# A hand-written order for the first tokens of a SwiGLU: norms, block differences and first products on four engines

## The chip, the cores and the metric

The kernel runs on one core of a Trainium2 chip. The metric is the device time of one execution, in microseconds (us); the median of three runs stands for a kernel. A core has a matrix engine (TensorE, PE in the profile), a vector engine (VectorE, DVE), an activation engine (ScalarE, ACT), a general engine (GpSimd, POOL) and a queue that issues most of the transfers (SyncE, SP). Each engine works through its own list of instructions in the order in which the program holds them; engines wait for each other through semaphores.

## The reference, cut to what matters

One encoder layer on 1024 tokens of 1024 features. The change lies in the very first part, a SwiGLU of width 2816 behind an RMSNorm; the mixer and the second SwiGLU that follow are untouched.

```python
def rmsnorm(x, g):
    xf = x.astype(jnp.float32)
    y = xf * lax.rsqrt(jnp.mean(xf * xf, axis=-1, keepdims=True) + EPS)
    return (y * g.astype(jnp.float32)).astype(x.dtype)

def swiglu(x, w_gate, w_up, w_down):
    return (jax.nn.silu(x @ w_gate) * (x @ w_up)) @ w_down

def hybrid_layer(h, layer_idx, p):
    f = swiglu(rmsnorm(h, p["ffn1_pre_g"]), p["ffn1_w_gate"], p["ffn1_w_up"], p["ffn1_w_down"])
    h = h + 0.5 * rmsnorm(f, p["ffn1_post_g"])
    m = hybrid_mixer(rmsnorm(h, p["mix_pre_g"]), layer_idx, p)
    ...
```

## The kernel before, in words

Float32 operands are kept as two parts, a rounded one and the rest of it ("high" and "low"): `split` (L171 to L173) makes the high part on ACT and the low part by a subtraction on DVE, or on POOL where the caller names it. A product of two such operands is three matmuls (`mm3`, L178 to L180).

The first SwiGLU multiplies by blocks, with seven products in place of eight. The normed input has four blocks: first or last 512 tokens, first or last 512 features. For the seven products the kernel needs the transposed blocks b11 and b21 (both feature halves of the first 512 tokens), b22 (the last features of the last tokens) and four differences t1 to t4, which mix the blocks of first and last tokens. `blocks_prep` (L257) makes them, one tile of 128 tokens at a time. For every tile it loads x, squares and sums it on ACT and takes the power on POOL (`rstd`, L196 to L198), scales it on DVE (L264), transposes four 128x128 pieces at a time on PE (L270) and splits them. Tiles 0 to 3 have two such transposed groups (b11, b21). Tiles 4 to 7 have five (b22, t1 to t4) and before them four subtractions: t1 on POOL (L280), t2 on DVE (L281), t3 and t4 on POOL (L282, L283). The normed tiles 0 to 3 stay in two tiles of the weights' ring (`kept`); t1 and t2 lie in the two halves of the work tile w3, t3 and t4 in those of w4, x of tiles 4 to 7 takes turns in w0 and w1, and the gain lies in w2.

`begun` (called after tile 3) and `held` (after tiles 4 and 5) are the first products, those that need the first tokens alone. `begun` loads a weight tile of gate and one of up, splits each into two halves with the low parts on POOL, multiplies b11 by the first half, copies that sum out on ACT (`u`, L344), adds the product of b21 and the second half in the same bank of PSUM, and takes SiLU (L330) and the product with up (L334). `held` multiplies b11 by the first halves of the weight tiles 1 and 2, and leaves the four sums in their banks. One such product with a block is 12 matmuls of 128x512; all of these are 96. Transposes use banks 0 to 3 in turn.

Then the loop of `matrix` takes one weight tile pair after another: POOL adds and subtracts its quarters (L368 to L371), ACT and DVE split them, PE multiplies. Weight tiles come through three buffers for raw weights, so a load waits until the low part of an earlier tile has been made.

What sets the order: the program is built with a scheduler that follows a model of the engines' times, and places every instruction on its engine's list itself; the order of the Python calls only breaks ties. Nothing in the first SwiGLU is ordered by hand.

Of the kernel before, what the change touches and what calls it, by code (L numbers as in the profile page):

```python
# [17 lines left out]
F32 = mybir.dt.float32  # L18
# [3 lines left out]
ALU = mybir.AluOpType  # L22
# [3 lines left out]
P = 128  # L26
D = 1024
# [65 lines left out]
class Tags:  # L93


    def __init__(self, pool, n):
        self.pool, self.n = pool, n
        self.place = dict(x=(0, 2), gain=(2, 1), t0=(3, 1, 0), t1=(3, 1, 1), t2=(4, 1, 0), t3=(4, 1, 1))
        self.turn, self.made, self.half, self.next = {}, {}, None, 0

    def whole(self, i):
        return self.pool.tile([P, D], F32, tag=f"w{i}", name=f"w{i}", bufs=1)

    def tile(self, shape, dtype, tag, name, bufs):
        if tag == "rstd":
            return self.pool.tile(shape, dtype, tag=tag, name=name, bufs=bufs)
        if tag == "c":
            if self.half is None:
                self.half = self.whole(self.next % self.n)
                self.next += 1  # L110
                return self.half[:, 0:512]
            h, self.half = self.half, None
            return h[:, 512:1024]
        first, n, *part = self.place[tag]
        if not part:
            k = self.turn[tag] = (self.turn.get(tag, -1) + 1) % n
            return self.whole(first + k)
        if part[0] == 0:
            self.made[first] = self.whole(first)
        return self.made[first][:, part[0] * 512:(part[0] + 1) * 512]  # L120
# [17 lines left out]
class Kernel:  # L138
# [118 lines left out]
    def blocks_prep(self, tags, kept, junk, ps, src, gain, C, t):  # L257
# [44 lines left out]
    def blocks_gate_up(self, ring, cp, spool, ps, C, wg, wu, gd, early):  # L302
# [34 lines left out]
        def begun(i):  # L337

            for w in (wg, wu):
                r = raw(w[i])  # L340
                p = bank()
                u = spool.tile([P, 512], F32, tag="u", name="u", bufs=2)
                product(p, unit(r[:, 0:512], G), "b11")
                A.copy(out=u, in_=p)  # L344
                product(p, unit(r[:, 512:1024], G), "b21", True)
                first.append((u, None, None))
                if w is wg:
                    sg = gate11(p, spool.tile([P, 512], F32, tag="s", name="s", bufs=3))
                else:
                    up11(p, sg, i)  # L350

        def held(i, banks):

            for w, b in zip((wg, wu), banks):
# [4 lines left out]
                first.append((None, p, b))  # L359

# [948 lines left out]
def build(tc, a, out, stages="all"):  # L1309
    nc = tc.nc  # L1310
    with ExitStack() as top:
# [26 lines left out]
        with ExitStack() as c1:  # L1338
            ps = Banks(k.pool(c1, "ps1", space=PSUM))
            with ExitStack() as cb:  # L1340
# [7 lines left out]
                def early(begun, held):  # L1348
                    g = tags.tile([P, D], F32, "gain", "gain", 1)
                    nc.sync.dma_start(out=g, in_=a["ffn1_pre_g"].partition_broadcast(P))  # L1350
# [4 lines left out]

                    ps.turn = [0, 1, 2, 3]
# [191 lines left out]
```

## Time and profile before

| | |
|---|---|
| median of three runs | 2636.75 us (2634.49 to 2637.43) |
| the profiled execution's own time | 2636.05 us |
| its span, first to last instruction | 2634.3 us |
| PE busy | 2523.7 us (96%) |
| DVE, ACT, POOL busy | 1521.7, 1003.9, 825.1 us |
| mean granted clock of PE | 0.985 |

The profiled execution is 0.70 us under the median. PE is the busiest engine by far, so a stretch in which it waits, or in which it is granted the lower of its clocks, is what a change of order can move. In the profile's rows a time is counted from the span's start; a row gives the start, the duration, engine, line, operation, what is written and read, and in brackets how long the engine stood idle before it and what ended that. PEclk 1.00 is 2.4 GHz, 0.50 is 1.2 GHz.

### The profile page before, as it was taken

What the parts mean: (1) busy time and instruction counts of PE and PEld (TensorE: products, weight loads), DVE (VectorE), ACT (ScalarE), POOL (GpSimd) and SP (SyncE); (2) the same over time, 40 slices, a digit from 0 to 9 for tenths busy, and PEclk for the clock granted to TensorE, in tenths of its full rate; (3) what the DMA queues carried; (4) which work ended last, traced back from release to release, by engine and by line L of the source; (5) the groups of instructions that cost most, each with busy time, mean ns of one, the idle gap of its engine ahead of it and who ended that gap; (6) DMA issues with size and microseconds to landing.
All of it is one profiled execution on the core that took longest, in us unless ns stands there. A gap on an engine that the chain in (4) does not pass through costs nothing.

```text
span 2634.3 us, 32969 instructions
## 1 busy us (share of the span) xinstructions
PE 2523.7 (96%) x12504; PEld 2122.4 (81%) x12504; DVE 1521.7 (58%) x2123; ACT 1003.9 (38%) x1709; POOL 825.1 (31%) x750
## 2 busy tenths in 40 slices
PE   6999999999999999999979999999999999999996
PEld 4888888888888898877757888888888888888885
DVE  5765654564746553777737888888723333333336
ACT  5333222344535533454426555555531111111113
POOL 6432321020210484344326666666400000000005
PEclk8999999999999999999989999999999999999998
DMA  3322222765722575555464444441421111111112
GB/s 140 102 79 80 96 76 77 242 201 179 253 95 89 174 244 205 165 185 183 138 172 110 117 112 121 105 141 60 170 70 35 48 48 48 49 48 48 48 41 104
DMA packets 133694, 309.60 MB, mean 118 GB/s; under 512 B 13728, under 2 KB 62752, under 8 KB 128672
## 3 DMA queue, kind: packets, MB, share of 16 engines
q1 hardware_dynamic: 115200, 245.89, 28.3%
q0 software_dynamic: 10016, 57.42, 8.1%
q10 hardware_dynamic: 8320, 4.19, 0.5%
q8 instruction: 98, 1.61, 0.3%
q14 instruction: 60, 0.49, 0.1%
HBM read 228.02 MB, written 79.43 MB: 117 GB/s over the span
## 4 chain that ended last, share of the span: by engine, by line
PE 82%; DVE 6%; POOL 3%; ACT 3%; issue 2%; DMA 2%; SPq 0%; DVEq 0%; POOLq 0%; ACTq 0%
PE po L180 7%; PE po L178 7%; PE po L179 7%; PE b L178 5%; PE b L179 5%; PE b L180 5%; PE pp L178 5%; PE pp L180 5%; PE pp L179 5%; PE pg L178 3%; PE pg L179 3%; PE pg L180 3%; PE pu L179 3%; PE pu L178 3%; PE pu L180 3%
## 5 line engine op out<-in xcount | busy, mean ns | idle before, releaser
L197 POOL TENSOR_SCALAR rstd<-rstd 128x1 f32<-128x1 f32 x64 | 32.2, 503 | 986.8 <-ACT junk L196 985.8
L173 DVE TENSOR_TENSOR split<-raw,split 128x1024 fp32r<-128x1024 f32 (+3 forms) x218 | 250.3, 1154 | 128.4 <-ACT split L172 127.6
L172 ACT CAST split<-raw 128x1024 fp32r<-128x1024 f32 (+3 forms) x227 | 192.8, 860 | 231.0 <-issue 77.4
L502 DVE TENSOR_TENSOR acc<-acc,po 128x512 f32<-128x512 f32 x160 | 108.6, 686 | 209.6 <-PE po L180 209.5
L1046 ACT ACTIVATE e<-sc,st 128x1024 f32<-128x1024 f32 x128 | 143.4, 1120 | 165.4 <-DVE st L1042 165.4
L178 PE MATMUL pp<-hT,split 128*128 128x512 f32 x384 | 153.6, 400 | 10.2 <-DVE o L911 10.2
L1042 DVE TENSOR_REDUCE st<-sc 128x1 f32<-128x1024 f32 x128 | 150.6, 1217 | 12.6 <-PE sc L1040 12.6
L180 PE MATMUL pp<-hT,split 128*128 128x512 f32 x384 | 152.0, 396 | 0.0
L179 PE MATMUL pp<-hT,split 128*128 128x512 f32 x384 | 151.8, 395 | 0.0
L178 PE MATMUL po<-odd,g 128*128 128x512 f32 x352 | 139.0, 397 | 6.8 <-DVE acc L502 6.8
L180 PE MATMUL po<-odd,g 128*128 128x512 f32 x352 | 138.4, 395 | 0.0
L179 PE MATMUL po<-odd,g 128*128 128x512 f32 x352 | 138.2, 393 | 0.0
L178 PE MATMUL b<-hT,split 128*128 128x512 f32 x352 | 137.0, 390 | 0.0
L179 PE MATMUL b<-hT,split 128*128 128x512 f32 x352 | 136.9, 389 | 0.0
L180 PE MATMUL b<-hT,split 128*128 128x512 f32 x352 | 136.9, 389 | 0.0
L1053 POOL TENSOR_SCALAR e<-e,st 128x768 f32<-128x768 f32 x64 | 75.6, 1181 | 181.5 <-DVE st L1052 136.7
L179 PE MATMUL po<-split,gs 128*128 128x512 f32 x334 | 131.9, 395 | 0.0
L180 PE MATMUL po<-split,gs 128*128 128x512 f32 x334 | 131.9, 395 | 0.0
L178 PE MATMUL po<-split,gs 128*128 128x512 f32 x334 | 131.3, 395 | 0.0
L172 ACT CAST g<-sg 128x512 fp32r<-128x512 f32 (+1 forms) x52 | 28.8, 553 | 243.7 <-DVE acc L502 124.8
L1055 POOL TENSOR_TENSOR e<-e,e 128x768 f32<-128x768 f32 x64 | 118.3, 1848 | 5.4
L178 PE MATMUL pp<-split,hT 128*128 128x512 f32 (+1 forms) x320 | 117.5, 368 | 0.0
(378 smaller groups left out, 7246.7 us busy)
## 6 DMA issues: line engine op xcount, KB each, us to landing
raw<-in_w_down_dram SPq DMA_DIRECT2D x88, 512.0 KB
raw<-in_w_gate_dram SPq DMA_DIRECT2D x45, 512.0 KB
raw<-in_w_up_dram SPq DMA_DIRECT2D x45, 512.0 KB
qkd<-o SPq DMA_DIRECT2D x64, 256.0 KB
qk<-qkd POOLq DMA_DIRECT2D x16, 1024.0 KB, 7.8
gd<-w SPq DMA_DIRECT2D x42, 256.0 KB
vd<-o SPq DMA_DIRECT2D x32, 256.0 KB
kb<-qkd POOLq DMA_DIRECT2D x16, 512.0 KB, 5.2
```

Source lines behind the costliest of these rows:

```text
L172: self.nc.scalar.copy(out=hi, in_=src)
L173: (eng or self.nc.vector).tensor_tensor(out=lo, in0=src, in1=hi.bitcast(F32), op=ALU.subtract)
L178: mm(out=out, lhsT=a[0], rhs=b[0], start=start, stop=False, **kw)
L179: mm(out=out, lhsT=a[0], rhs=b[1], start=False, stop=False, **kw)
L180: mm(out=out, lhsT=a[1], rhs=b[0], start=False, stop=stop, **kw)
L197: nc.gpsimd.tensor_scalar(out=r[:, 1:2], in0=r[:, 0:1], scalar1=k / n, scalar2=k * EPS, op0=ALU.mult, op1=ALU.add)
L502: nc.vector.tensor_tensor(out=a[:, ns], in0=a[:, ns], in1=po[n], op=ALU.add)
L1042: nc.vector.tensor_reduce(out=X["st"][:, j:j + 1], in_=pc, op=ALU.max, axis=AX.X, negate=True)
L1046: self.nc.scalar.activation(out=X["e", j], in_=X["sc", j], func=AF.Exp, bias=st[:, j:j + 1], accum_out=st[:, 2 + j:3 + j])
L1053: G.tensor_scalar(out=e1[:, XD:], in0=e1[:, XD:], scalar1=st[:, 5:6], scalar2=0.0, op0=ALU.mult, op1=ALU.add)
L1055: G.tensor_tensor(out=e0[:, XD:], in0=e0[:, XD:], in1=e1[:, XD:], op=ALU.add)
```

## The change

Four things change. First, `blocks_prep` becomes a generator with two stops (after the norm's sums, and after the differences), its x is loaded by the caller, and the order of all calls is written out by hand inside `tc.manual_schedule` for PE, ACT, DVE and POOL; there the scheduler keeps the order of the calls. SP's queue is still the scheduler's. Second, `begun` is cut into load, begin, end and out, and `held` into its two products, and these stand between the tiles: gate's two products before the groups of tile 4, up's before those of tile 5, one of tile 1's products before tile 6 and the other before tile 7, the two of tile 2 behind tile 7. Third, the differences take the place of what they are made of: t1 and t4 overwrite the two halves of the kept tile, t3 the first half of x, and only t2 has a tile of its own. That leaves a third work tile for x. Fourth, the first tile of x is loaded ahead of the gain.

```diff
@@ class Tags
-        self.place = dict(x=(0, 2), gain=(2, 1), t0=(3, 1, 0), t1=(3, 1, 1), t2=(4, 1, 0), t3=(4, 1, 1))
-        self.turn, self.made, self.half, self.next = {}, {}, None, 0
+        self.place = dict(x=(0, 3), gain=(3, 1), t2=(4, 1))
+        self.turn, self.half, self.next = {}, {}, 0
...
@@ blocks_prep
-    def blocks_prep(self, tags, kept, junk, ps, src, gain, C, t):
+    def blocks_prep(self, tags, x, y, ps, gain, C, t, junk=None):
...
-        x = kept[t] if t < 4 else tags.tile([P, D], F32, "x", "x", 2)
-        nc.sync.dma_start(out=x, in_=src[t * P:(t + 1) * P, :])
-        r = self.rstd(tags, x, junk=junk())
+        r = self.rstd(tags, x, junk=junk and junk())
+        yield
         V.scalar_tensor_tensor(out=x, in0=x, scalar=r, in1=gain, op0=ALU.mult, op1=ALU.mult)
...
-        y = kept[t - 4]
-        t1, t2, t3, t4 = (tags.tile([P, 512], F32, f"t{i}", f"t{i}", 1) for i in range(4))
-        G.tensor_tensor(out=t1, in0=x0, in1=y[:, 0:512], op=ALU.subtract)
+        t1, t2, t3, t4 = y[:, 0:512], tags.tile([P, 512], F32, "t2", "t2", 2), x0, y[:, 512:1024]
+        G.tensor_tensor(out=t1, in0=x0, in1=t1, op=ALU.subtract)
         V.tensor_tensor(out=t2, in0=x1, in1=t1, op=ALU.subtract)
         G.tensor_tensor(out=t3, in0=x1, in1=x0, op=ALU.subtract)
-        G.tensor_tensor(out=t4, in0=y[:, 512:1024], in1=t2, op=ALU.subtract)
+        G.tensor_tensor(out=t4, in0=t4, in1=t2, op=ALU.subtract)
+        yield
         for n, v in (("b22", x1), ("t1", t1), ("t2", t2), ("t3", t3), ("t4", t4)):
             turn(n, v)
@@ blocks_gate_up
+            def load(self):
+                r = raw(self.w[self.i])
+                self.a11 = unit(r[:, 0:512], G)
+                self.a12 = unit(r[:, 512:1024], G)
+            def begin(self):
+                self.p = ps.at(4 if self.other is None else 5, [P, 512], "b")
+                self.u = spool.tile([P, 512], F32, tag="u", name="u", bufs=2)
+                product(self.p, self.a11, "b11")
+                A.copy(out=self.u, in_=self.p)
+                first.append((self.u, None, None))
+            def end(self):
+                product(self.p, self.a12, "b21", True)
...
@@ early
+                    xs = [load(0)]
                     g = tags.tile([P, D], F32, "gain", "gain", 1)
                     nc.sync.dma_start(out=g, in_=a["ffn1_pre_g"].partition_broadcast(P))
...
-                    for t in range(T):
-                        k.blocks_prep(tags, kept, junk, ps, a["x"], g, C, t)
-                        if t == 3:
-                            begun(0)
-                        elif t in (4, 5):
-                            held(t - 3, (2 * t - 4, 2 * t - 3))
+                    xs += [load(t) for t in range(1, 4)]
...
+                    with tc.manual_schedule(engines={E.PE, E.Activation, E.DVE, E.Pool}):
+                        for t in (0, 1, 0, 2, 1, 3, 2):
+                            step(t)
+                        gate, up = begun(0)
+                        gate.load()
+                        step(3)
+                        gate.begin()
+                        step(4)
+                        up.load()
+                        gate.end()
+                        for t in (5, 4):
+                            step(t)
+                        gate.out()
+                        step(4)
+                        up.begin()
+                        for t in (6, 5):
+                            step(t)
+                        up.end()
+                        step(5)
+                        up.out()
+                        for t in (7, 6):
+                            step(t)
+                        gate, up = held(1, (6, 7))
+                        gate()
+                        for t in (6, 7):
+                            step(t)
+                        up()
+                        step(7)
+                        for one in held(2, (4, 5)):
+                            one()
```

The change moves three lists where the prediction looks. In the lists below L173, L178 to L180, L196 to L198, L264, L270 and L280 to L283 of the kernel before are L175, L180 to L182, L198 to L200, L266, L272 and L281 to L284 of the changed one.

DVE at its first instructions, before: `split_111` and `split_112` hold the tiles 0 to 3, `hT0_98` is where b11 and b21 are split to, `pt` a transposed group.

```order
L264 SCALAR_TENSOR_TENSOR split_111<-split_111,rstd_115,w2_109 128x1024
L264 SCALAR_TENSOR_TENSOR split_111<-split_111,rstd_136,w2_109 128x1024
L264 SCALAR_TENSOR_TENSOR split_112<-split_112,rstd_157,w2_109 128x1024
L173 TENSOR_TENSOR hT0_98<-pt_120,hT0_98 128x4x128
L264 SCALAR_TENSOR_TENSOR split_112<-split_112,rstd_178,w2_109 128x1024
L173 TENSOR_TENSOR hT0_98<-pt_127,hT0_98 128x4x128
```

And DVE at the same place now.

```order
L266 SCALAR_TENSOR_TENSOR split_109<-split_109,rstd_120,w3_112 128x1024
L175 TENSOR_TENSOR hT0_98<-pt_130,hT0_98 128x4x128
L175 TENSOR_TENSOR hT0_98<-pt_137,hT0_98 128x4x128
L266 SCALAR_TENSOR_TENSOR split_109<-split_109,rstd_125,w3_112 128x1024
L175 TENSOR_TENSOR hT0_98<-pt_150,hT0_98 128x4x128
L175 TENSOR_TENSOR hT0_98<-pt_157,hT0_98 128x4x128
L266 SCALAR_TENSOR_TENSOR split_110<-split_110,rstd_145,w3_112 128x1024
```

The scaling of a tile now stands behind both low parts of the tile ahead of it; before, three tiles were scaled in a row.

POOL between the low parts of the first weights and the first difference, before: `split_201` and `split_237` are the weights of `begun`, `split_321` and `split_405` those of `held`, `w0` and `w1` the tiles 4 and 5.

```order
L173 TENSOR_TENSOR split_201<-raw_197,split_201 128x512 x2
L173 TENSOR_TENSOR split_237<-raw_233,split_237 128x512 x2
L173 TENSOR_TENSOR split_321<-raw_318,split_321 128x512
L173 TENSOR_TENSOR split_321<-raw_336,split_321 128x512
L173 TENSOR_TENSOR split_405<-raw_402,split_405 128x512
L173 TENSOR_TENSOR split_405<-raw_420,split_405 128x512
L197 TENSOR_SCALAR rstd_272<-rstd_272 128x1
L198 TENSOR_TENSOR rstd_272<-rstd_272,mhalf_65 128x1
L197 TENSOR_SCALAR rstd_356<-rstd_356 128x1
L198 TENSOR_TENSOR rstd_356<-rstd_356,mhalf_65 128x1
L280 TENSOR_TENSOR w3_277<-w0_269,split_111 128x512
```

And POOL now, from the norm of tile 7 (`rstd_376`) on: `w2_312` is tile 6, `w0_373` tile 7, `split_389` the weights of the first call of `held`.

```order
L199 TENSOR_SCALAR rstd_376<-rstd_376 128x1
L200 TENSOR_TENSOR rstd_376<-rstd_376,mhalf_65 128x1
L281 TENSOR_TENSOR split_110<-w2_312,split_110 128x512
L283 TENSOR_TENSOR w2_312<-w2_312 128x512
L284 TENSOR_TENSOR split_110<-split_110,w4_381 128x512
L175 TENSOR_TENSOR split_389<-raw_386,split_389 128x512
L281 TENSOR_TENSOR split_110<-w0_373,split_110 128x512
L283 TENSOR_TENSOR w0_373<-w0_373 128x512
L284 TENSOR_TENSOR split_110<-split_110,w4_381 128x512
L175 TENSOR_TENSOR split_389<-raw_444,split_389 128x512
```

All eight low parts of the first weights stood ahead of the first difference; now those of `held` stand behind the differences of tile 6 and of tile 7.

PE around the groups of tiles 5 to 7, before: `hT_98` is b11 or b21, `t_100` the block t2, with which the first full weight matrix begins.

```order
L180 MATMUL b<-hT_98,split 128x512
L270 MATMUL pt<-ident,w_278 128x128 x4
L270 MATMUL pt<-ident,w_353 128x128 x4
L270 MATMUL pt<-ident,w_361 128x128 x8
L270 MATMUL pt<-ident,w_362 128x128 x8
L270 MATMUL pt<-ident,w_437 128x128 x4
L270 MATMUL pt<-ident,w_445 128x128 x8
L270 MATMUL pt<-ident,w_446 128x128 x8
L270 MATMUL pt<-ident,w_486 128x128 x4
L270 MATMUL pt<-ident,w_494 128x128 x8
L270 MATMUL pt<-ident,w_495 128x128 x8
L178 MATMUL b<-t_100,split 128x512
```

And PE now: the end of up's products, the five groups of tile 5, and the beginning of `held`'s first product, whose third matmul (L182) is the first that reads a low part from POOL.

```order
L182 MATMUL b<-hT_98,split 128x512
L272 MATMUL pt<-ident,w_247 128x128 x4
L272 MATMUL pt<-ident,split 128x128 x4
L272 MATMUL pt<-ident,w_255 128x128 x4
L272 MATMUL pt<-ident,w_247 128x128 x4
L272 MATMUL pt<-ident,split 128x128 x4
L180 MATMUL b<-hT_98,split 128x512
L181 MATMUL b<-hT_98,split 128x512
L182 MATMUL b<-hT_98,split 128x512
```

Before, 96 products came first and then the groups of four tiles; now 12 or 24 products stand between the groups of two tiles, and the groups of the later tile are behind them on PE's list.

## Rows read from the trace of the kernel before

**Rows 1.** The page's busy time: engine, us, share of the span, instructions.

```profile
PE 2523.7 (96%) x12504; PEld 2122.4 (81%) x12504; DVE 1521.7 (58%) x2123; ACT 1003.9 (38%) x1709; POOL 825.1 (31%) x750
```

**Rows 2.** Busy time of each engine by stretch, with PE's granted clock.

```profile
core 0: us, PE busy (x) PEld busy (x) DVE busy (x) ACT busy (x) POOL busy (x), PEclk, DMA share, GB/s
0.00:20.93 20.93, 7.17 (x33) 5.99 (x33) 9.89 (x12) 12.08 (x21) 12.24 (x20) 0.92 0.68 251
20.93:46.00 25.07, 24.93 (x122) 20.71 (x122) 10.28 (x11) 9.63 (x16) 13.89 (x13) 0.99 0.36 116
46.00:52.00 6.00, 2.43 (x19) 1.75 (x18) 4.34 (x6) 4.25 (x8) 3.29 (x5) 0.99 0.24 87
52.00:71.04 19.04, 9.78 (x40) 7.47 (x41) 16.99 (x19) 9.57 (x17) 16.42 (x13) 0.50 0.17 57
71.04:2634.30 2563.26, 2479.44 (x12298) 2086.54 (x12296) 1480.20 (x2078) 968.34 (x1648) 779.29 (x702) 0.99 0.37 117
```

**Rows 3.** Timeline of ACT: norms of the first tiles, casts, one copy, the last norm.

```profile
7.23 1.06 ACT L196 ACTIVATE junk<-split 128x1024 bf16<-128x1024 f32 x1 [5.15 <-DMA split<-in_x_dram]
8.54 1.06 ACT L196 ACTIVATE junk<-split 128x1024 bf16<-128x1024 f32 x1 [0.16 <-DMA split<-in_x_dram]
19.43 0.59 ACT L172 CAST hT<-pt 128x512 fp32r<-128x512 f32 x1 [2.12 <-PE pt L270]
20.29 0.59 ACT L172 CAST hT<-pt 128x512 fp32r<-128x512 f32 x1 [0.27 <-PE pt L270]
27.07 0.59 ACT L344 COPY u<-b 128x512 f32<-128x512 f32 x1 [0.32 <-PE b L180]
52.21 1.06 ACT L196 ACTIVATE junk<-w 128x1024 bf16<-128x1024 f32 x1 [0.21 <-DMA w<-in_x_dram]
```

**Rows 4.** Timeline of DVE: scalings alone and beside POOL, a low part, a difference.

```profile
9.32 1.28 DVE L264 SCALAR_TENSOR_TENSOR split<-split,rstd,w 128x1024 f32<-128x1024 f32 x1 [9.32 <-POOL rstd L198]
15.34 2.28 DVE L264 SCALAR_TENSOR_TENSOR split<-split,rstd,w 128x1024 f32<-128x1024 f32 x1
20.05 0.69 DVE L173 TENSOR_TENSOR hT<-pt,hT 128x512 fp32r<-128x512 f32 x1
45.44 0.69 DVE L281 TENSOR_TENSOR w<-w,w 128x512 f32<-128x512 f32 x1
```

**Rows 5.** Timeline of POOL: one norm, one difference; SP's loads of tiles 6 and 7.

```profile
8.46 0.19 POOL L197 TENSOR_SCALAR rstd<-rstd 128x1 f32<-128x1 f32 x1 [7.06 <-ACT junk L196]
8.74 0.55 POOL L198 TENSOR_TENSOR rstd<-rstd,mhalf 128x1 f32<-128x1 f32 x1
42.74 1.29 POOL L283 TENSOR_TENSOR w<-split,w 128x512 f32<-128x512 f32 x1 [0.63 <-DVE w L281]
42.81 6.46 SPq L262 DMA_DIRECT2D w<-in_x_dram  x2
```

**Rows 6.** Timeline of PE: first group, groups at either clock, products at either clock.

```profile
10.67 3.90 PE L270 MATMUL pt<-ident,split 128*128 128x128 f32 x16 [10.67 <-DVE split L264]
18.28 2.82 PE L270 MATMUL pt<-ident,split 128*128 128x128 f32 x12 [2.34 <-DVE hT L173]
45.10 1.91 PE L270 MATMUL pt<-ident,w 128*128 128x128 f32 x16
71.61 0.63 PE L179 MATMUL b<-t,split 128*128 128x512 f32 x1
72.04 0.56 PE L180 MATMUL b<-t,split 128*128 128x512 f32 x1
72.67 0.40 PE L179 MATMUL b<-t,split 128*128 128x512 f32 x1
72.91 0.39 PE L180 MATMUL b<-t,split 128*128 128x512 f32 x1
```

**Rows 7.** Busy time at the start of the second SwiGLU, columns as in rows 2.

```profile
1820.00:1840.00 20.00, 18.66 (x120) 16.41 (x119) 14.65 (x25) 9.15 (x18) 11.84 (x13) 1.00 0.19 67
1840.00:1860.00 20.00, 14.27 (x66) 10.55 (x65) 18.84 (x23) 9.51 (x17) 11.64 (x12) 1.00 0.54 191
```

More of the change, by code (lines that the diff above doesn't have):

```diff
@@ L97, in __init__, with halves @@
         self.pool, self.n = pool, n
-        self.place = dict(x=(0, 2), gain=(2, 1), t0=(3, 1, 0), t1=(3, 1, 1), t2=(4, 1, 0), t3=(4, 1, 1))
-        self.turn, self.made, self.half, self.next = {}, {}, None, 0
+        self.place = dict(x=(0, 3), gain=(3, 1), t2=(4, 1))
+        self.turn, self.half, self.next = {}, {}, 0
     def whole(self, i):
         return self.pool.tile([P, D], F32, tag=f"w{i}", name=f"w{i}", bufs=1)
+    def halves(self, tag, place):
+        if self.half.get(tag) is None:
+            self.half[tag] = self.whole(place())
+            return self.half[tag][:, 0:512]
+        return self.half.pop(tag)[:, 512:1024]
     def tile(self, shape, dtype, tag, name, bufs):
@@ L107, in tile, with place @@
         if tag == "c":
-            if self.half is None:
-                self.half = self.whole(self.next % self.n)
+            def place():
                 self.next += 1
[L111 to L120, printed above, removed]
+                return (self.next - 1) % self.n
+            return self.halves(tag, place)
+        first, n = self.place[tag]
+        if tag == "t2":
+            return self.halves(tag, lambda: first)
+        k = self.turn[tag] = (self.turn.get(tag, -1) + 1) % n
+        return self.whole(first + k)
 class Banks:
@@ L337, in begun, with __init__, out, one @@
         def begun(i):
[L339 to L348, printed above, removed]
+            gate, up = Begun(wg, i), Begun(wu, i)
+            gate.other, up.other = None, gate
+            return gate, up
+        class Begun:
+            def __init__(self, w, i):
+                self.w, self.i = w, i
+            def load(self):
[10 more added lines that the diff above has]
+                product(self.p, self.a12, "b21", True)
+            def out(self):
+                if self.other is None:
+                    self.sg = gate11(self.p, spool.tile([P, 512], F32, tag="s", name="s", bufs=3))
                 else:
-                    up11(p, sg, i)
+                    up11(self.p, self.other.sg, self.i)
         def held(i, banks):
-            for w, b in zip((wg, wu), banks):
+            def one(w, b):
                 r = ring.load(1024)[:, 0:512]
@@ L359, in held @@
                 first.append((None, p, b))
+            return [lambda w=w, b=b: one(w, b) for w, b in zip((wg, wu), banks)]
         def matrix(w, i, final):
@@ L1348, in early @@
                 def early(begun, held):
-                    g = tags.tile([P, D], F32, "gain", "gain", 1)
-                    nc.sync.dma_start(out=g, in_=a["ffn1_pre_g"].partition_broadcast(P))
                     kept = [r.bitcast(F32)[:, i, :] for r in (ring.take(1024) for _ in range(2)) for i in range(2)]
@@ L1354, in junk, with load @@
                         return spool.tile([P, D], BF16, tag="s", name="junk", bufs=3)
+                    def load(t):
+                        x = kept[t] if t < 4 else tags.tile([P, D], F32, "x", "x", 3)
+                        nc.sync.dma_start(out=x, in_=a["x"][t * P:(t + 1) * P, :])
+                        return x
                     ps.turn = [0, 1, 2, 3]
-                    for t in range(T):
-                        k.blocks_prep(tags, kept, junk, ps, a["x"], g, C, t)
-                        if t == 3:
-                            begun(0)
-                        elif t in (4, 5):
-                            held(t - 3, (2 * t - 4, 2 * t - 3))
+                    xs = [load(0)]
@@ new lines, in early, with step @@
+                    g = tags.tile([P, D], F32, "gain", "gain", 1)
+                    nc.sync.dma_start(out=g, in_=a["ffn1_pre_g"].partition_broadcast(P))
+                    xs += [load(t) for t in range(1, 4)]
+                    prep = []
+                    def step(t):
+                        if t == len(xs):
+                            xs.append(load(t))
+                        if t == len(prep):
+                            prep.append(k.blocks_prep(tags, xs[t], kept[t - 4], ps, g, C, t, junk))
+                        next(prep[t], None)
```

1 line of the change is left out of this document (added).

## The prediction, made before the changed kernel was run

> **What bounds the kernel now.** I read the page's busy times first: PE works 2523.7 of 2634.3 us [rows 1]. Then the stretches: after 71.04 us PE works 2479.4 of 2563.3 us at clock 0.99, but before that only 7.2 of 20.9, 24.9 of 25.1, 2.4 of 6.0 and 9.8 of 19.0 us, the last at clock 0.50, that is 1.2 GHz [rows 2]. So in the first 71 us PE stands idle 13.8 us until its first product at 20.93 and 12.8 us between 46 and 71.04, where the groups of tiles 4 to 7 come one by one and no product is left to put between them. At 71.04 all groups and all 96 matmuls of the first products are done, and PE goes on without a gap. That moment is my milestone: the work up to it is the same in both orders, PE is full behind it, and a shift of it goes to the end of the kernel undiminished. Last I read the timelines for prices.
>
> **Prices.** From the start of a tile's square to its scaling on DVE 2.1 us (7.23 on ACT [rows 3], 9.32 on DVE [rows 4], the norm on POOL between [rows 5]). Scaling 1.28 us, but 2.28 where POOL is in the middle of a subtraction: the two wait for one another [rows 4]. Scaling to PE's first transpose 1.35 (9.32 [rows 4] to 10.67 [rows 6]). A group of four transposes 0.47 at the full clock (1.91 for 16) and 0.94 at half (2.82 for 12) [rows 6]; at half, the cast starts 1.15 after the group (18.28 [rows 6], 19.43 [rows 3]), the next group's 0.86 later [rows 3]. Cast to low part 0.62 (19.43 [rows 3], 20.05 [rows 4]), low part 0.69 [rows 4]. A difference or low part on POOL 1.29, t2 on DVE 0.69 [rows 5, 4]. A matmul of a product 0.23 to 0.24 at full clock and 0.43 at half, by the starts of neighbours [rows 6]: 12 are 2.8 or 5.2 us.
>
> **The change part by part.** Each engine's count of instructions stays as it was; what changes is what stands in front of what. I lay the new lists along these prices.
>
> *Tiles 0 to 3.* The first x is loaded ahead of the gain. Two loads land 1.31 us apart (starts of the first two squares [rows 3]), so the first scaling comes at 8.0 in place of 9.32; the gain, now second, has landed by then. But a scaling now stands behind both low parts of the tile ahead of it: 1.35 + 1.15 + 0.62 + 0.86 + 0.69 = 4.7 us per tile, one after the other. Tile 3 is scaled at 8.0 + 3 x 4.7 + 1.0 (POOL is at the weights' low parts) = 23.0, its transposes start at 24.4 and take 1.9, and the first product starts at 26.3 in place of 20.93: +5.4.
>
> *Gate's products.* The first 12 start at half clock, say 3.4 us, to 29.7. The second half adds to the same bank, so PE waits for the copy (0.59 [rows 3] and the way there and back: 0.85). In the old order other products stood in that gap. Then 12 more, to 33.3.
>
> *Tile 4.* Its square stands behind that copy: 30.4, norm done 32.5. On POOL the low parts of up's weights and tile 5's norm stand ahead of t1, and the scaling waits for one of them: scaling 33.8 to 35.0, t1 37.1, t2 38.5, t3 39.1, t4 40.4 to 41.6. PE ends the fifth group at 42.3. From 33.3 to 42.3 it does 2.3 us of work (five groups): 6.5 us waiting, the rest half clock.
>
> *Up's products and tile 5.* 2.8 + 0.85 + 2.8, to 48.6. t1 of tile 5 stands behind tile 6's norm on POOL, whose square stands behind up's copy (45.9): t1 48.0, t4 ends 52.4, fifth group 52.9: 1.9 us waiting.
>
> *The first product of `held`.* POOL makes its low part only behind tile 7's norm and tile 6's three differences: square of tile 7 at 53.7, norm done 56.7 (tile 6's scaling in between), t1 57.9, t3 59.8, t4 61.1, low part 62.4. PE can do two of twelve matmuls, then the third waits for that low part. Behind it on PE stand tile 6's groups, and ACT and DVE wait for those. PE's work from 52.9 to 66.3 is 2.8 us (3.9 with the first ones at half clock): 9.1 us waiting.
>
> *Tile 6 and the second product of `held`.* The groups of tile 6, long ready, stood behind that product: 66.3 to 68.8. Tile 7's scaling stands behind their low parts, 70.6; t1 73.1, t2 73.8, t3 75.1, t4 76.3, and the weights' low part behind these 77.6. The remaining ten matmuls at half clock: 82.0. 8.4 us waiting.
>
> *Tile 7 and the rest.* Groups to 84.9, low parts of the last two weights 87.9 and 89.2, products to 93.0: 2.6 us waiting.
>
> The sum: 93.0 against 71.04, +22.0. By kind: +5.4 at the first product; from there 96 matmuls and 20 groups at full clock are 31.5 us in both. The new order adds 30 us of waits (1.7 for the copies, 6.5, 1.9, 9.1, 8.4, 2.6) and 5 us of half clock; the old one had 18.6 us of both together (71.04 - 20.93 - 31.5). Laid along the old lists, the same prices bring the milestone to 72.8, 1.7 late; I take that off. The raw weights have three buffers, and the loads of the first full matrix now wait for `held`'s low parts, at 77.6 and later, so behind the milestone I add 0.9 for its first low parts on DVE. +21.2 on 2636.05 is 2657.3 for the execution shown; on the median, which is 0.70 above it, 2658.
>
> **What costs nothing.** Differences in place of their tiles: the same twelve subtractions; a reader and a later writer of a half are on POOL in order or far apart. The third tile for x brings tile 6's load to the start; before, tiles 6 and 7 were loaded from 42.81 on, and only tile 7's square waited for it, 0.21 us [rows 3, 5]. Tile 7's load now follows tile 4's groups: the second of the old issues ended at 49.27 and the square began at 52.21, some 3.3 us after it was issued [rows 3, 5]; from 41.7 that is 45, and its square stands at 53.7, so 8 us of cover. On SP's list `held`'s last weights stand behind the first store, which goes at 55; they are needed at 86. Bounds for both: 0.2 gained, 3 lost.
>
> The scheduler also moves a few instructions at the start of the second SwiGLU, since its own clock is shifted there. PE waits 1.3 + 5.7 us in that stretch [rows 7]; I take 0, between 3 gained and 3 lost.
>
> **A rule against part of the sum.** Groups and products in turn spread PE's work, and in the trace the clock fell to 0.50 where groups came alone and stayed there until the products at 71 us [rows 2, 6]. The Trainium skill, "TensorE: Matmul & The Clock Gate", Part 1, says of the gate that the default state is throttled and activity releases the throttle; by it, products between the groups should hold the clock up, and this trace has no such mixture to show it. As a mechanism of this kernel: the 5 us of half clock in my sum go, 2658 - 5 = 2653.
>
> **Rivals.**
> Clock up: as above, 2653. For it, products are dense for 2.8 to 5.6 us at a time; against it, PE is idle about half of the stretch by my own sum, more than where the clock fell.
> Late weights: loads that were issued at 23 us go out at 77 to 98, each some 3.3 us from issue to use, with POOL, ACT and DVE behind them; where two of those lie open, +6: 2664. For it, three buffers and no slack; against it, PE has 24 products to do meanwhile.
> The holes are filled: what the order could do if POOL were ahead. If the low parts of `held` stood ready when PE reached them and tile 4's differences came without the wait, 6.5 + 9.1 + 8.4 + 2.6 us and the half clock would go: 93.0 - 26.6 - 5 = 61.4, ten before 71.04: 2627. It decides at the third matmul of `held`: ready or not. POOL's list says not, since the three differences of a tile stand in front, and behind tile 7's square, which ends only at 54.9, two us after PE has arrived.
> Smaller parts: a stretch that hides more than I see (tile 0 to 3 overlapping, tile 4 earlier), +5 to +12: about 2645.
>
> **How the numbers follow.** Forecast as summed 0.66, clock up 0.15, late weights 0.11, smaller 0.04, filled 0.03, no difference 0.01. 0.2% of this kernel is 5.3 us, about what its measurement tells from no change. All but the last two cases are over that on the slow side: slower 0.95, same 0.015, faster 0.035. The range: below, clock up with 3 us gained in the second SwiGLU and a little more hidden, 2648; above, late weights and 3 us lost there, 2667.
>
> **What would show it.** First product near 26 us; DVE's list with 4.6 us from scaling to scaling; PE's longest waits for POOL at the low parts of `held` (6 to 7 us each, the third matmul of twelve), the clock at 0.50 in parts of the stretch up to 90; the 96th matmul ending near 92. A first product before 21 or a milestone before 71 makes the forecast wrong in sign; waits of PE on POOL under 3 us each make its main term wrong.

## The result and the profile after

The changed kernel takes 2662.03 us (median, 2660.87 to 2665.57) beside 2636.56 for the kernel before: ratio 1.0100, 95% interval 1.0083 to 1.0118, so 25.5 us slower. The forecast was 2658, range 2648 to 2667. The two profiled executions, 2660.87 (the shortest of the four) and 2636.05 us, are 24.8 us apart; the accounts below are between these two.

Busy time by stretch in the profile after, cut at the steps of the prediction (columns as in [rows 2]):

```profile
core 0: us, PE busy (x) PEld busy (x) DVE busy (x) ACT busy (x) POOL busy (x), PEclk, DMA share, GB/s
0.00:25.16 25.16, 7.64 (x33) 6.28 (x33) 10.21 (x12) 10.81 (x18) 8.46 (x18) 1.00 0.59 219
25.16:33.00 7.84, 7.17 (x25) 4.94 (x24) 2.39 (x3) 4.19 (x8) 1.80 (x3) 1.00 0.09 33
33.00:41.23 8.23, 4.24 (x21) 3.18 (x21) 3.96 (x6) 4.34 (x8) 7.39 (x7) 0.79 0.11 32
41.23:48.00 6.77, 6.09 (x30) 4.69 (x29) 2.57 (x3) 2.22 (x4) 1.92 (x3) 1.00 0.25 80
48.00:65.18 17.18, 7.73 (x32) 5.41 (x31) 6.45 (x9) 4.39 (x8) 10.21 (x9) 0.70 0.09 31
65.18:80.94 15.76, 7.73 (x33) 5.75 (x32) 5.02 (x7) 3.54 (x7) 5.46 (x4) 0.71 0.10 34
80.94:92.21 11.27, 9.02 (x46) 6.94 (x44) 3.19 (x6) 4.68 (x9) 4.44 (x4) 0.95 0.30 93
92.21:2659.10 2566.89, 2479.46 (x12297) 2085.50 (x12296) 1482.33 (x2081) 970.76 (x1649) 782.21 (x705) 0.99 0.37 117
```

The last row answers to the last of [rows 2]: behind the milestone PE does the same work, 2479.46 us against 2479.44, in 2566.89 us against 2563.26. So 21.2 of the 24.8 us are lost ahead of the milestone (92.21 against 71.04) and 3.6 behind it.

The scalings of tiles 0 to 3 on DVE's timeline after (start, us, engine, line, operation):

```profile
7.19 1.28 DVE L266 SCALAR_TENSOR_TENSOR split<-split,rstd,w 128x1024 f32<-128x1024 f32 x1 [7.19 <-POOL rstd L200]
11.76 1.28 DVE L266 SCALAR_TENSOR_TENSOR split<-split,rstd,w 128x1024 f32<-128x1024 f32 x1
16.32 1.28 DVE L266 SCALAR_TENSOR_TENSOR split<-split,rstd,w 128x1024 f32<-128x1024 f32 x1
20.95 2.30 DVE L266 SCALAR_TENSOR_TENSOR split<-split,rstd,w 128x1024 f32<-128x1024 f32 x1
```

They are 4.57 us apart, one after the other. The first comes 2.1 us earlier than in [rows 4], the first product (25.16) 4.2 us later than before.

PE's timeline after, around the two products of the first held pair:

```profile
25.16 0.79 PE L180 MATMUL b<-hT,split 128*128 128x512 f32 x1
...
54.10 0.50 PE L180 MATMUL b<-hT,split 128*128 128x512 f32 x1 [2.23 <-ACT split L174]
54.45 0.44 PE L181 MATMUL b<-hT,split 128*128 128x512 f32 x1
60.98 0.80 PE L182 MATMUL b<-hT,split 128*128 128x512 f32 x1 [6.09 <-POOL split L175]
61.57 0.63 PE L180 MATMUL b<-hT,split 128*128 128x512 f32 x1
...
65.18 0.60 PE L272 MATMUL pt<-ident,w 128*128 128x128 f32 x4
...
69.41 0.50 PE L180 MATMUL b<-hT,split 128*128 128x512 f32 x1 [1.57 <-ACT split L174]
69.75 0.40 PE L181 MATMUL b<-hT,split 128*128 128x512 f32 x1
76.51 0.80 PE L182 MATMUL b<-hT,split 128*128 128x512 f32 x1 [6.36 <-POOL split L175]
```

And POOL's timeline in the same stretch:

```profile
55.39 1.25 POOL L281 TENSOR_TENSOR split<-w,split 128x512 f32<-128x512 f32 x1
...
58.45 1.25 POOL L284 TENSOR_TENSOR split<-split,w 128x512 f32<-128x512 f32 x1
59.67 1.25 POOL L175 TENSOR_TENSOR split<-raw,split 128x512 fp32r<-128x512 f32 x1
70.91 1.26 POOL L281 TENSOR_TENSOR split<-w,split 128x512 f32<-128x512 f32 x1 [9.99 <-DVE w L266]
...
73.98 1.25 POOL L284 TENSOR_TENSOR split<-split,w 128x512 f32<-128x512 f32 x1
75.20 1.25 POOL L175 TENSOR_TENSOR split<-raw,split 128x512 fp32r<-128x512 f32 x1
```

And DVE's, from tile 6's low parts to tile 7's scaling:

```profile
66.44 1.29 DVE L175 TENSOR_TENSOR hT<-pt,hT 128x512 fp32r<-128x512 f32 x2 [9.07 <-ACT hT L174]
67.64 1.93 DVE L175 TENSOR_TENSOR t<-pt,t 128x512 fp32r<-128x512 f32 x3
69.49 1.28 DVE L266 SCALAR_TENSOR_TENSOR w<-w,rstd,w 128x1024 f32<-128x1024 f32 x1
```

PE does two matmuls of each product and stands at the third, whose low part (L175) is the last of four on POOL, behind tile 6's differences the first time and tile 7's the second (L281, L283, L284). Between the two POOL stood idle 9.99 us for tile 7's scaling, which stood on DVE behind tile 6's low parts, whose groups stood on PE behind the first of those third matmuls. A ring of four lists: each engine waits with work ready behind what it waits for.

### The profile page after: what moved, and what is told of

Read it like the earlier page. It is cut to its first block, busy times and chain, and to the rows that moved or that the text cites. A ratio compares the mean times of both kernels' runs of the same rounds, so it can differ in the third digit from the quotient of the medians.

```text
span 2659.1 us, 32964 instructions
## 1 busy us (share of the span) xinstructions
PE 2529.1 (95%) x12504; PEld 2122.7 (80%) x12504; DVE 1516.1 (57%) x2123; ACT 1004.9 (38%) x1709; POOL 821.9 (31%) x750
## 4 chain that ended last, share of the span: by engine, by line
PE 80%; DVE 7%; POOL 4%; ACT 4%; issue 3%; DMA 3%; SPq 0%; DVEq 0%; POOLq 0%; ACTq 0%
PE po L182 6%; PE po L180 6%; PE po L181 6%; PE b L180 5%; PE b L182 5%; PE b L181 5%; PE pp L180 5%; PE pp L182 5%; PE pp L181 5%; PE pg L180 3%; PE pu L181 3%; PE pu L180 3%; PE pg L181 3%; PE pu L182 3%; PE pg L182 3%
## 5 line engine op out<-in xcount | busy, mean ns | idle before, releaser
L175 DVE TENSOR_TENSOR split<-raw,split 128x1024 fp32r<-128x1024 f32 (+3 forms) x218 | 248.1, 1144 | 133.6 <-ACT split L174 132.7
L180 PE MATMUL pp<-hT,split 128*128 128x512 f32 x384 | 153.5, 400 | 10.6 <-DVE o L930 10.6
L182 PE MATMUL b<-hT,split 128*128 128x512 f32 x352 | 139.5, 396 | 13.6 <-POOL split L175 13.1
L182 PE MATMUL pp<-hT,split 128*128 128x512 f32 x384 | 151.9, 396 | 0.0
L180 PE MATMUL b<-hT,split 128*128 128x512 f32 x352 | 139.6, 397 | 6.7 <-ACT split L174 5.4
L180 PE MATMUL po<-odd,g 128*128 128x512 f32 x352 | 138.7, 396 | 7.1 <-DVE acc L521 7.0
L181 PE MATMUL b<-hT,split 128*128 128x512 f32 x352 | 138.9, 395 | 0.0
L182 PE MATMUL po<-odd,g 128*128 128x512 f32 x352 | 138.1, 394 | 0.0
L182 PE MATMUL po<-split,gs 128*128 128x512 f32 x334 | 131.9, 395 | 0.0
L180 PE MATMUL po<-split,gs 128*128 128x512 f32 x334 | 131.1, 395 | 0.0
L180 PE MATMUL pp<-split,hT 128*128 128x512 f32 (+1 forms) x320 | 117.7, 368 | 0.0
```

The lines of the kernel that those rows point to most:

```text
L175: (eng or self.nc.vector).tensor_tensor(out=lo, in0=src, in1=hi.bitcast(F32), op=ALU.subtract)
L180: mm(out=out, lhsT=a[0], rhs=b[0], start=start, stop=False, **kw)
L181: mm(out=out, lhsT=a[0], rhs=b[1], start=False, stop=False, **kw)
L182: mm(out=out, lhsT=a[1], rhs=b[0], start=False, stop=stop, **kw)
```

## The experiments

All times are medians in us, of 4 to 11 executions; before ran beside each batch at 2636.04, 2635.93, 2635.77 and 2635.31.

| run | time | range | ratio to before |
|---|---|---|---|
| early_weights | 2646.22 | 2644.53 to 2647.30 | 1.0039 (1.0027 to 1.0052) |
| tiles_ahead | 2657.45 | 2654.32 to 2659.62 | 1.0081 (1.0068 to 1.0095) |
| scheduler_order | 2624.08 | 2623.69 to 2626.58 | 0.9958 (0.9945 to 0.9972) |
| filled_waits | 2657.34 | 2654.24 to 2660.57 | 1.0082 (1.0068 to 1.0096) |
| old_order_new_parts | 2640.89 | 2637.76 to 2642.53 | 1.0018 (1.0009 to 1.0027) |
| new_order_old_parts | 2630.11 | 2626.70 to 2633.73 | 0.9981 (0.9972 to 0.9989) |
| gpsimd_list_only | 2633.09 | 2629.61 to 2635.80 | 0.9989 (0.9980 to 0.9998) |
| vector_list_only | 2646.01 | 2644.73 to 2646.76 | 1.0040 (1.0027 to 1.0053) |
| own_order | 2622.76 | 2621.36 to 2623.97 | 0.9952 (0.9938 to 0.9965) |
| all_but_vector | 2648.95 | 2647.76 to 2651.34 | 1.0051 (1.0039 to 1.0064) |
| old_order_2 | 2636.55 | 2633.59 to 2639.64 | 1.0006 (0.9997 to 1.0015) |
| own_order_2 | 2620.17 | 2617.55 to 2620.98 | 0.9941 (0.9928 to 0.9953) |

**early_weights.** The split inside `held` becomes a step of its own:

```diff
-                p = ps.at(b, [P, 512], "b")
-                product(p, unit(r, G), "b11")
+                u = unit(r, G)
+                yield
+                p = ps.at(b, [P, 512], "b")
+                product(p, u, "b11")
...
+gate, up = held(1, (6, 7))
+next(gate)
 for t in (7, 6): step(t)
-gate, up = held(1, (6, 7))
-gate()
-for t in (6, 7): step(t)
-up()
+next(gate); step(6); next(up); step(7); next(up)
```

> The changed kernel, but the two weight blocks of the first held pair are cast and get their low parts one step earlier: gate's ahead of tile 7's norm and tile 6's differences, up's ahead of tile 7's differences. The products stay where they are. Theory (TensorE's two longest waits, 6.1 and 6.4 us, are only the place of these low parts in GpSimd's list): both waits shrink below 1 us, the milestone (96th matmul of the first products and all groups done) comes 11 to 13.5 us earlier, near 79 to 81, and the time falls from 2662 to 2648 to 2651. Rival (tile 7's norm and tile 6's differences only take the place of the low parts as what ends last, so TensorE waits as long at the groups): 2658 to 2662.

Measured 2646.22. PE's timeline of this run at the same two matmuls:

```profile
54.67 0.53 PE L182 MATMUL b<-hT,split 128*128 128x512 f32 x1 [0.62 <-POOL split L175]
...
64.23 0.50 PE L182 MATMUL b<-hT,split 128*128 128x512 f32 x1 [0.62 <-POOL split L175]
...
79.00 0.50 PE L180 MATMUL b<-hT,split 128*128 128x512 f32 x1
```

Both waits fall from over 6 to 0.62 us and the milestone comes at 79.00 in place of 92.21: 13.2 us of the 21.2, as the theory said. The time is 2 us under its range: the second SwiGLU took 3.0 us less here than in the changed kernel, for a reason of its own (old_order_2, below). The places of two subtractions in POOL's list, and of their casts in ACT's, cost more than half of the loss.

**tiles_ahead.** In tiles 0 to 3 the step ends behind the scaling and behind the first group as well, and the calls are `(0, 1, 0, 2, 0, 1, 0, 3, 1, 2, 1, 2, 3, 2)` before the first weights.

> The changed kernel, but in tiles 0 to 3 each scaling stands on VectorE ahead of the second low part of the tile before it, and the groups follow in between. Theory (first product late because a scaling stands behind both low parts of the tile ahead): a tile takes 3.7 us in place of 4.6, the first product comes 3 to 3.5 us earlier, near 22, everything behind it shifts by the same, and the time falls to 2658 to 2659. Rival (the start is hidden by GpSimd's later list, as a late start only eats into later waits): first product earlier, milestone unchanged at 92, 2661 to 2662.

Measured 2657.45, but not by the theory's way. Two rows of PE's timeline in the profiled run, the first product and the first behind the milestone:

```profile
22.60 0.79 PE L180 MATMUL b<-hT,split 128*128 128x512 f32 x1
...
91.66 0.50 PE L180 MATMUL b<-hT,split 128*128 128x512 f32 x1
```

The first product is 2.6 us earlier, the milestone 0.55: the first nine matmuls now ran slowly (0.79 to 0.58 us in the records, up to 26.9), and both long waits were as long as before. DVE's last copy out of the first SwiGLU's sums (`f<-po`) begins at 742.43, against 741.39 in the changed kernel: in this run nothing of the early start is left there, and it ends earlier only because the second SwiGLU took 3.2 us less, again for the reason found in old_order_2. The profiled run is the slowest of the four, so how the median's 4.6 us divide stays open.

**scheduler_order.** One line: `with tc.manual_schedule(...)` becomes `if True:`.

> The changed kernel without the fixed order: the same instructions, sums in place of their tiles, the first x ahead of the gain and three x tiles, and the scheduler free to order all engines. Theory (the whole loss is the fixed order, the other edits cost nothing): not slower than before, 2625 to 2638; the first product near 21. Rival (the sums in place of their tiles or the third x tile make part of the loss, by waits for a tile that is still being read): 2642 to 2655.

Measured 2624.08, 12 us faster than before, 0.9 under the theory's range, and 38 faster than the changed kernel with the very same calls. From its first product on, at 22.09, PE works 35.42 of 39.91 us (columns as in [rows 2]):

```profile
22.09:62.00 39.91, 35.42 (x177) 29.56 (x176) 30.79 (x37) 23.01 (x41) 39.06 (x31) 0.92 0.29 100
```

The fixing of the lists costs 38 us, not 25; the new parts and the new order of calls, left free, gain 12.

**filled_waits.** Ahead of both products of the first held pair:

```diff
+z = ps.at(4, [P, 512], "b")
+for j in range(32):
+    nc.tensor.matmul(out=z, lhsT=busy[0][:, 0:P], rhs=C["b11"][:, 0, 0, :], start=j == 0, stop=j == 31)
```

> The changed kernel with 32 matmuls into an unused bank (start and stop of their own, nothing reads them) ahead of each of the two products of the first held pair, some 7.3 us of TensorE's work laid into waits of 9.1 and 8.7 us; the output is the same. Theory (the clock at 0.50 behind these two waits costs TensorE about 2 us each, and it falls because TensorE stands idle): the clock stays near 1.0 from 48 to 80 us, the milestone comes 3 to 5 us earlier, 2657 to 2659. Rival (the half clock costs nothing, since GpSimd's list ends last anyway): 2661 to 2663.

Measured 2657.34. Its stretches (columns as in [rows 2]):

```profile
53.00:66.00 13.00, 11.46 (x61) 9.28 (x60) 3.98 (x6) 2.95 (x7) 7.22 (x6) 1.00 0.12 40
66.00:80.00 14.00, 12.38 (x63) 9.81 (x61) 5.17 (x8) 3.72 (x9) 5.56 (x4) 1.00 0.12 39
80.00:95.00 15.00, 13.65 (x52) 10.54 (x53) 6.86 (x7) 4.53 (x9) 8.49 (x6) 0.89 0.37 113
```

The first matmul behind the milestone on PE's timeline:

```profile
88.58 0.39 PE L180 MATMUL b<-hT,split 128*128 128x512 f32 x1
```

With useless work in the waits the clock stays at 1.00 through both, where it was 0.70 and 0.71, and the milestone comes at 88.58 in place of 92.21, 3.6 us earlier, as the theory said. So the half clock behind the waits is a cost of its own. The 4.7 us between the medians (2657.34 against 2662.03) do not measure it. Behind the milestone PE now waits 1.48 us at 98.47 and 1.45 us at 100.66, and DVE's last copy out of the first SwiGLU's sums begins at 739.45 against 741.39, only 1.9 us earlier; the second SwiGLU then took 3.2 us less, for the reason found in old_order_2.

**old_order_new_parts and new_order_old_parts.** The first calls the parts in the old order, free:

```diff
-with tc.manual_schedule(engines={E.PE, E.Activation, E.DVE, E.Pool}):
-    ...
+for t in range(T):
+    for _ in range(3): step(t)
+    if t == 3:
+        for m in begun(0): m.load(); m.begin(); m.end(); m.out()
+    elif t in (4, 5):
+        for one in held(t - 3, (2 * t - 4, 2 * t - 3)): one()
```

> The changed kernel's parts (sums in place of their tiles, three x tiles, first x ahead of the gain, norms and products as separate steps), but called in the order of the kernel before, tile by tile, and left to the scheduler. Theory (these parts cost and bring nothing; what counts is the order alone): within 3 us of before, 2633 to 2639, PE's first product at 20 to 22 us. Rival (the gain of the scheduler's run over before, 12 us, comes from these parts, three x tiles and tiles freed early above all): 2622 to 2628.

The second is scheduler_order with two x tiles, tiles of their own for t1 to t4, and the gain first:

> The counterpart: the changed kernel's order of calls, left to the scheduler, but with the parts of before (two x tiles, tiles of their own for the sums, the gain loaded ahead of the first x). Theory (the order in which the code asks for norms, scalings, weights and products is worth some 10 us as long as no engine is bound to it): 2623 to 2628. Rival (the order is worth nothing, the parts are): 2633 to 2639.

Measured 2640.89 and 2630.11: both outside what was expected. The new order with the old parts is 5.8 us faster than before, the old order with the new parts 5.0 slower, both together 12 faster. The two runs with the new order differ by 6.0 us, most of it in the first SwiGLU: DVE's last copy out of its sums begins at 714.06 with the old parts and at 708.76 with the new. The 5.0 needed a test of its own (old_order_2, below).

**gpsimd_list_only, vector_list_only, all_but_vector.** One line each: `engines={E.Pool}`, `engines={E.DVE}`, `engines={E.PE, E.Activation, E.Pool}`.

> The changed kernel with only GpSimd's list fixed; the scheduler orders TensorE, VectorE and ScalarE. Theory A (TensorE's two waits of 6 us come from GpSimd's list alone, so fixing it alone keeps them): 2640 or more, with a wait of 5 us or more on a low part of the first held pair. Theory B (a list costs this only where the lists in front of it are fixed too, since a fixed VectorE holds back tile 6's and 7's scalings, and these GpSimd's differences): 2625 to 2631, no such wait.

> The changed kernel with only VectorE's list fixed. Theory A (GpSimd's list is the cause): like the scheduler's run, 2623 to 2628. Theory B (VectorE's list is the one that binds: each scaling stands behind the low parts of groups that wait for TensorE, so a wait of TensorE comes back a tile later as a wait of all four engines): 2642 to 2652, with the groups of tiles 6 and 7 after 75 us.

> The changed kernel's order with the lists of TensorE, ScalarE and GpSimd fixed and VectorE left to the scheduler. Theory A (VectorE's fixed list alone binds): 2624 to 2632. Theory B (the loss comes from lists that wait for one another, and TensorE's and GpSimd's still do): 2644 to 2653, with a wait of over 3 us of TensorE for GpSimd at a low part of the first held pair.

Measured 2633.09, 2646.01, 2648.95 (none fixed 2624.08, all four 2662.03). PE's waits from 22 to 110 us by sum, how often and the longest, for gpsimd_list_only (the first two):

```profile
PE pt L272 <- DVE t L175: 1.7, 1, 1.7
PE pt L272 <- POOL w L283: 1.1, 1, 1.1
```

for vector_list_only (the first two):

```profile
PE pt L272 <- DVE split L266: 6.2, 1, 6.2
PE pt L272 <- DVE w L282: 3.9, 3, 1.5
```

and for all_but_vector (the first two):

```profile
PE b L182 <- POOL split L175: 7.0, 3, 5.8
PE b L180 <- ACT split L174: 5.4, 3, 2.2
```

With POOL's list alone fixed the order that I had named as the cause is there in full, and the wait is not: no wait over 1.7 us. (Its time is still 2 us over theory B's range; it has the bad order in the second SwiGLU described below.) With DVE free one of the two long waits stays (5.8 us), the other is gone. Theory B of both other runs came out: DVE's list alone costs 22 us, the other three without it 25, all four 38. Counted to DVE's last copy out of the first SwiGLU's sums, where the second SwiGLU plays no part (708.76 with no list fixed, 713.23 with POOL's, 728.33 with DVE's, 732.32 with the other three, 741.39 with all four), these are 4.5 for POOL's list, 19.6, 23.6 and 32.6. So the loss belongs to no single list. What a list costs depends on which others are fixed: DVE's alone costs 19.6 us, and freeing it among the four gives back 9.1. PE's and ACT's list alone, and pairs of lists, were not run, so which two close the ring stays open.

**own_order.** All four lists fixed as in the changed kernel, in another order, with steps that also end behind the scaling and behind every group, and some low parts on DVE (V). Digits are steps of tiles; L and l make weights, B, E, O and p are products and what follows them:

```diff
-for t in (0, 1, 0, 2, 1, 3, 2): step(t)
-...
+for s in ("0 0 1 2 3 1 0 2 1 3 Lg1v Lu1v 2 2 Lg2 3 4 3 4 0 5 1 5 Bg 4 l1g Lu2v 4 Bu 6 Eg 4 5 Og 4 4 "
+          "5 Eu 5 l1u 6 5 Ou 4 5 5 7 6 6 p1g 7 6 l2gv 7 p1u l2u 6 7 7 p2g 6 7 6 p2u 7 7").split():
+    do[s]() if s in do else step(int(s))
```

> The changed kernel's parts with all four lists still fixed, but in another order: tile 0 whole to its scaling first, four norms and scalings ahead of the groups, low parts of the first gate and up blocks on VectorE while it stands idle, every weight block at least one tile ahead of its product, and the groups of tiles 4 to 7 laid between the products one or two at a time. Theory (a fixed order is no loss in itself; what costs is a waiting instruction with ready work behind it): no wait of TensorE over 2 us after the first product, milestone (groups and products of the stretch) some 19 us ahead of before's, 2614 to 2622. Rival (four fixed lists lock together whatever their order, since a slip in one passes to all): above 2630.

> The kernel of the run old_order_new_parts, with the norm of tile 5 asked for one place earlier in the program. All lists are the same as there up to the start of the second SwiGLU; there the scheduler now puts two sums that are ready (they read TensorE's banks) ahead of a scaling that waits for its norm on VectorE, as in the kernel before, where old_order_new_parts had them behind it. Theory (the 5 us that old_order_new_parts is slower than before are this wait of TensorE for a bank, and the half clock behind it): 3 to 5 us faster than old_order_new_parts, 2635 to 2638, clock near 0.97 in the first 20 us there in place of 0.82. Rival (the new parts themselves cost, in the first stretch): 2640 to 2642.

> The kernel of the run own_order with tile 7's scaling two places later in its fixed order; in the second SwiGLU the scheduler now puts the two ready sums ahead of the waiting scaling on VectorE. The first stretch is 0.5 us longer at most. Theory (own_order gives back 2 to 4 us of its lead at that wait of 3.4 us): 2618 to 2621. Rival (the lead is lost elsewhere between the first SwiGLU and the end): 2622 to 2624.

Measured 2622.76, 2636.55 and 2620.17. In own_order, behind 20 us, PE's waits show one (2.19 us) before 110; a fixed order is no loss in itself. Its median is 0.8 us over the range. The first matmul behind the milestone comes at 54.53, 16.5 us ahead of before where 19 were expected, and the second SwiGLU loses some 3 us by the same cause as the 5.0 us above. On DVE's timeline of own_order, at the start of the second SwiGLU:

```profile
1831.05 3.37 DVE L208 SCALAR_TENSOR_TENSOR qk<-acc,rstd,qk 128x1024 f32<-128x1024 f32 x1 [2.32 <-POOL rstd L200]
1834.34 0.74 DVE L1332 SCALAR_TENSOR_TENSOR acc<-pgu,vv,acc 128x512 f32<-128x512 f32 x1
```

of own_order_2:

```profile
1830.30 0.74 DVE L1332 SCALAR_TENSOR_TENSOR acc<-pgu,vv,acc 128x512 f32<-128x512 f32 x1
1831.37 0.75 DVE L1332 SCALAR_TENSOR_TENSOR acc<-pgu,vv,acc 128x512 f32<-128x512 f32 x1 [0.33 <-PE pgu L182]
1832.71 3.42 DVE L208 SCALAR_TENSOR_TENSOR qk<-acc,rstd,qk 128x1024 f32<-128x1024 f32 x1 [0.59 <-POOL rstd L200]
```

In the first a scaling that waits for its norm stands ahead of two sums that are ready, and those sums read the banks that PE wants: PE waits 3.37 us in own_order and 0.71 in own_order_2 at that matmul, and does 51 against 65 matmuls in 20 us at clock 0.83 against 1.00:

```profile
1826.00:1846.00 20.00, 14.48 (x51) 10.78 (x52) 17.68 (x20) 9.42 (x17) 9.90 (x12) 0.83 0.56 185
```

```profile
1827.00:1847.00 20.00, 14.42 (x65) 10.86 (x66) 19.08 (x23) 10.62 (x17) 12.71 (x13) 1.00 0.54 191
```

old_order_2 is old_order_new_parts with `if t == 4: step(5)` in the loop. Its lists differ at this place and behind it, and in one cast of ACT at the start (16.70 us there, 19.23 here); it reaches the second SwiGLU 3.0 us later. Two points of the chain that ended last, one at the start of the second SwiGLU and one 54.6 us ahead of the end of either, for old_order_new_parts:

```profile
1843.50 2.14 DVE mhl L175
2585.35 3.41 DVE acc L1531
```

and for old_order_2:

```profile
1846.49 2.06 DVE mhl L175
2582.80 3.41 DVE acc L1533
```

741.85 us against 736.31, 5.5 less, and the median is 4.3 us lower, level with before. So in the old order the new parts cost nothing that the medians tell from noise, and this one pair of places is worth 5.5 us here; own_order_2 takes 2.8 us less than own_order from the start of the second SwiGLU to the end. (The clock that I expected there, 0.97, came only 20 us later: 0.83 in the first 20 us, then 1.00 where old_order_new_parts had 0.84.) own_order_2 is the fastest kernel of all: 15 us under before, 42 under the changed one, with the same instructions, four low parts on DVE in place of POOL. (Its first SwiGLU ends 1.5 us later than in own_order, where 0.5 at most was expected.)

Which order a kernel has at this place bears on the runs above. The changed kernel, gpsimd_list_only, old_order_new_parts and own_order have the scaling first; before and the other runs have the two sums first. From DVE's last copy out of the first SwiGLU's sums to the end of the span the four take 1917.3 to 1920.4 us, the others 1913.5 to 1916.8. So some 3 us by which early_weights, tiles_ahead, filled_waits and scheduler_order are faster than the changed kernel come from here and not from the first SwiGLU.

## Why the prediction was right, and where it was off

The main step, adding up waits along the new lists, held. Step by step (forecast, then measured):

- First product 26.3, 25.16; per tile 4.7, 4.57. The first scaling was mis-sized: 8.0, but 7.19. That is most of the 1.1 us by which the first product came early. The distance of two loads of x (1.31 us) was taken for what the gain's load costs in front of them; the first square began 2.17 us earlier (5.06 against 7.23).
- Gate's products to 33.3, 33.0; copies 0.85 each, 0.68 as idle time (0.84 and 0.83 by the starts of the matmuls on either side).
- Tile 4's groups take 9.0 us, 8.2; of it waits of 6.5, 4.0 (8.23 less 4.24 busy), the rest slower groups at clock 0.79, to which the prediction gave next to nothing. Up and tile 5 10.6, 10.7 (to 51.9).
- First held product 13.4 us, 13.3, of it waits of 9.1, 8.3 (2.23 + 6.09). (The prediction's own parts, 9.1 and 3.9, fall 0.4 short of its 13.4.) Tile 6 and the second 15.7, 15.8, waits 8.4, 7.9. Tile 7 and the rest 11.0, 11.3.
- Half clock 5 us over the whole stretch; filled_waits, which filled two of its waits, brought the milestone 3.6 us forward.
- The milestone 93.0 raw, 92.21. The 1.7 us that I took off for lateness made it 0.9 too early: the error of the old lists' reckoning, whose working the prediction does not show, did not carry over.
- Behind the milestone 0.9 forecast, 3.6 measured. This is the term that failed in size. To the end of the first SwiGLU 1.3 us are lost (PE waits 0.53 at 93.47 for DVE's low part and 0.82 at 136.29), in the mixer 0.6, in the second SwiGLU 1.8, which I had put at 0 within 3. That the scheduler gives the changed kernel the worse order there is chance, for which the prediction had left 3 us. The changed kernel has the order shown above for own_order there; on PE's timeline after:

```profile
1874.44 0.80 PE L180 MATMUL pgu<-odd,mhl 128*128 128x512 f32 x1 [3.38 <-DVE acc L1320]
```

- That a shift of the milestone goes to the end undiminished did not hold to the microsecond: of 13.2 us at the milestone early_weights has 11.6 left at DVE's last copy out of the first SwiGLU's sums (729.83 against 741.39), of 3.6 filled_waits 1.9. Why early_weights loses the 1.6 stays open.

Of the rivals, clock up fell: 0.70 and 0.71 in the two worst stretches. (One argument against it does not come out of its rows: PE idle for a larger share than where the clock fell, but it is some 30 of 66.7 us by the sum and 9.3 of 19.0 in [rows 2].) Its rule did not: the Trainium skill, "TensorE: Matmul & The Clock Gate", Part 1, says that activity releases the throttle, and filled_waits agrees, 1.00 with work in the waits. Late weights fell too: POOL waits 2.04 to 3.50 us for raw weights from 90 to 110 us, and PE has no wait longer than 0.53 there. The chain that ended last does run through four of these loads from 96.29 to 125.62, and behind them PE waits the 0.82 us at 136.29; that is the size of it, where the rival said 6. The holes are filled named the right switch, the third matmul of `held`; early_weights threw it, for 13.2 us at the milestone of the 31.6 that the rival added up, since waits of about a microsecond (1.19, 1.47) stayed in front of each product and tile 4's stayed whole.

Where the reason was too narrow: I put the two long waits down to POOL's list, and gpsimd_list_only shows that list without them. The cause is several fixed lists at once. And "what costs nothing" was right only for the old order: with the new order of calls and the scheduler free the same parts bring 6 us (2630.11 to 2624.08).

## What to carry to other kernels

In a fixed list ask of each instruction that may wait: what is ready behind it, and which engine wants that. Two subtractions and their casts placed one tile earlier brought the milestone 13.2 us forward here; two sums placed ahead of one scaling were worth 2.8 and 5.5. Before blaming one engine's list, free the others: here PE waited for POOL, and with POOL's list alone fixed that wait was gone. And before crediting an edit with a time, look at the stretch that it was meant to move: with a scheduler at work, another stretch may have changed too.

## What was not expected of the hardware

In the changed kernel the long waits of PE are paid twice: behind the 6.09 us seven matmuls start 0.43 us apart (61.57 and 62.00 are the first two) in place of 0.23 before the clock is back, and behind the 6.36 us all that are left of the product (77.10 and 77.53 are the first two). With 64 matmuls that nothing reads in these waits the granted clock stayed at 1.00 and the milestone came 3.6 us earlier.
